# Differential and index scores in joint visits, upper and lower rows in turn

## The chip, the core and the metric

One core of a Trainium2 chip runs the whole kernel. The metric is the device time of one execution in microseconds, median of several; less is better.

## What is computed

Two layers of a decoder trunk on 256 tokens of width 2048, everything in float32. Each layer has a projection `w_in`, three kinds of attention heads side by side, an output projection, a cross attention and a feed-forward network. What matters here are the scores:

```python
# moba (6 heads, 128 wide) and dsa (6 heads, 128 wide): plain causal softmax attention,
# dsa only over the 64 keys that the index picks
# diff (4 heads): two components c of 64 columns each
sc = jnp.einsum('bqhcd,bshcd->bchqs', q, k) * scale
p = softmax(where(causal, sc, -inf))
a = p[:, 0] - lam * p[:, 1]
# index (8 heads of 64 columns): which keys dsa may see
rel = relu(jnp.einsum('bqhd,bsd->bqhs', qi, ki) * idx_scale)
score = jnp.einsum('bqhs,bqh->bqs', rel, w)
_, sel = lax.top_k(where(causal, score, -inf), 64)
```

With 256 tokens and blocks of 256, moba attends to its own block alone. There are 2 query tiles of 128 rows; tile `t = 0` sees 128 keys and tile `t = 1` sees 256 (`KW = (128, 256)`).

## The kernel before

**The main stream.** TensorE multiplies activations with streamed weights nearly all the time. A weight tile comes by DMA as float32 (`raw`, 4 buffers), ScalarE rounds it to a high half `hi` (L81, 4 buffers), VectorE forms the low half `lo = raw - hi` (L83, 3 buffers), and three matmuls replace one: `x_hi·hi`, `x_lo·hi`, `x_hi·lo` (L222, L223, L224 in `mm_rows` for the projections, L249 and L250 in `up_acc` for the rest). Outputs lie in 4 PSUM banks with the tag `mm`.

**The side work.** Everything about the heads (transposes, scores, softmax, products with the values, normalisation) is written as Python generators. `tick` (L159) is called by the main stream after every two blocks of `mm_rows`, or four of `up_acc`; it counts one and continues each generator that is due. `yield n` means "go on n ticks later". What a generator issues at one tick is called a visit below: on TensorE it stands between two matmuls of the main stream. The constants are in L32: `G_T` ticks from the end of a projection to its transposes, `G_S` from the transposes to the first scores, `G_PT` to the transposed probabilities, `G_DN` to the last transposes of the differential heads. Side work has 4 PSUM banks of its own, tag `at`, one for each call of `pat()`. The framework then orders every engine's instructions; an instruction that would wait can be placed a little behind main matmuls.

**Scores.** `softmax_pair` (L604) makes the scores of two units. For the plain heads a unit is one head with all 128 rows of contraction. For the differential heads a unit is one component `c` of one head: rows 0 to 63 of `qT` and `kT` for component 0, rows 64 to 127 for component 1. The second unit comes one tick after the first. Within a unit the two query tiles share one bank: matmul of `t = 0` (L618), masked maximum on VectorE (L620), then the same for `t = 1`. Since VectorE reads the bank that the second matmul writes, that matmul waits for the first L620.

**Index.** `index_masks` (L709) goes through the query tiles. The 8 index heads lie in four tiles of 128 rows, even heads in rows 0 to 63 and odd heads in rows 64 to 127. A group is four even or four odd heads for `t = 0`, two for `t = 1`, since 512 columns fill a bank. So there are 2 groups for `t = 0` and 4 for `t = 1`, each with a `yield 1`, a bank of its own, matmuls (L724), one Relu on ScalarE (L727) and a weighted sum on VectorE (L729).

**What follows.** 8 rounds of top-8 on VectorE (L734, L735) make the dsa mask, while the differential heads already run. After the last projection (`values(("mv", 2, 4))`, 8 ticks) the output projection `residual` starts; its first output block takes the mixed heads in the order 6 to 13, 14 and 15, 0 to 5 (one tick after each four blocks or at a group's end). Heads 4 and 5, the last moba pair, are its last operands. They come from `plain_pair`: product with the values (L665, L666), then `split` (L179: ScalarE L182, VectorE L186).

Of the kernel before, what the change touches and what calls it, by code (L numbers as in the profile page):

```python
# [13 lines left out]
AF = mybir.ActivationFunctionType  # L14
OP = mybir.AluOpType
AX = mybir.AxisListType

P = 128
D = 2048
S = 256  # L20
L = 2
NT = S // P
# [6 lines left out]
NEG = -1.0e30  # L29
GONE = -3.0e38  # L30
TOPK = 64
G_R, G_T, G_S, G_PT, G_DN = 5, 5, 1, 3, 3  # L32
FIRST_COL = 3328
KP, AP, RAWS, HIS, LOS = 38, 8, 4, 4, 3
SEVEN = frozenset((2, 5, 8, 11, 14, 16, 18))
# [8 lines left out]
def hybrid_trunk(ctx: ExitStack, tc: tile.TileContext, x, mem, positions, attn_norm, w_in,  # L44
# [3 lines left out]
    nc = tc.nc  # L48
# [9 lines left out]
    def slot(dt=F32):  # L58
        return kp.tile([P, CH], dt, tag="k", name="k", bufs=KP)
# [4 lines left out]
    def tmp():  # L64
        return tp.tile([P, CH], F32, tag="t", name="t", bufs=7)
# [4 lines left out]
    def pat():  # L70
        return ps.tile([P, CH], F32, tag="at", name="at")
# [41 lines left out]
    masks = [mask[:, P:], mask]  # L113
# [487 lines left out]
    KW = (P, S)  # L601
    PO = (0, P)

    def softmax_pair(units, mk, res, ri):  # L604


        mx = sp.tile([P, 2, NT], F32, tag="mx", name="mx")
        sm = sp.tile([P, 2, NT], F32, tag="sm", name="sm")
        for i, (qT, kT, lo, hi, sc) in enumerate(units):
            if i:  # L610
                yield 1
            pt = pat()
            s = tmp()
            p = slot()
            for t in range(NT):
                w = KW[t]
                o = pt[:, t * S:t * S + w]
                nc.tensor.matmul(o, lhsT=qT[lo:hi, t * P:(t + 1) * P], rhs=kT[lo:hi, :w],  # L618
                                 start=True, stop=True)
                nc.vector.tensor_tensor_reduce(out=s[:, PO[t]:PO[t] + w], in0=o, in1=mk[t], scale=1.0,  # L620
                                               scalar=GONE, op0=OP.add, op1=OP.max,
                                               accum_out=mx[:, i, t:t + 1])
            nb = sp.tile([P, NT], F32, tag="nb", name="nb")
            nc.vector.scalar_tensor_tensor(nb, mx[:, i, :], -1.0, sc, op0=OP.mult, op1=OP.mult)
            for t in range(NT):
                v = slice(PO[t], PO[t] + KW[t])
                nc.scalar.activation(p[:, v], s[:, v], AF.Exp, scale=sc[:, t:t + 1],
                                     bias=nb[:, t:t + 1], accum_out=sm[:, i, t:t + 1])
            res.append(p)
        nc.vector.reciprocal(ri, sm)  # L630
# [17 lines left out]
    def plain_pair(qTs, kTs, scs, mk, vs, mixT, base):  # L648

        while len(mk) < NT:  # L650
            yield 1
        prob, ri = [], new_ri()
        yield from softmax_pair([(qTs[i], kTs[i], 0, P, scs[i]) for i in range(2)], mk, prob, ri)
        for i in range(2):
            for t in range(NT):
                v = slice(PO[t], PO[t] + KW[t])
                nc.vector.tensor_scalar(prob[i][:, v], prob[i][:, v], ri[:, i, t:t + 1], None, op0=OP.mult)
        yield G_PT
        pTs = [p_T(prob[i]) for i in range(2)]
        yield 1  # L660
        while not vs():
            yield 1
        for i, v in enumerate(vs()):
            pt = pat()
            nc.tensor.matmul(pt[:, :S], lhsT=v[0], rhs=pTs[i][:, :S], start=True, stop=False)  # L665
            nc.tensor.matmul(pt[:, P:S], lhsT=v[1], rhs=pTs[i][:, S:3 * P], start=False, stop=True)  # L666
            mixT[base + i] = mix_slot(base + i)
            split((mixT[base + i], pt[:, :S], None))
# [40 lines left out]
    def index_masks(iqT, ikT, iw, res):  # L709

        accs = []
        for t in range(NT):
            w = KW[t]
            cur = slot()[:, :w]
            accs.append(cur)
            per = CH // w
            groups = [range(o, 8, 2) for o in range(2)]
            groups = [g[i:i + per] for i in range(0, 4, per) for g in groups]
            for hs in groups:
                yield 1  # L720
                pt = pat()
                for i, h in enumerate(hs):
                    lo = 64 * (h % 2)
                    nc.tensor.matmul(pt[:, i * w:(i + 1) * w], lhsT=iqT[h // 2][lo:lo + 64, t * P:(t + 1) * P],  # L724
                                     rhs=ikT[lo:lo + 64, :w], start=True, stop=True)
                rel = tmp()
                nc.scalar.activation(rel, pt, AF.Relu, scale=64 ** -0.5)  # L727
                for i, h in enumerate(hs):
                    nc.vector.scalar_tensor_tensor(cur, rel[:, i * w:(i + 1) * w], iw[t][:, h:h + 1],  # L729
                                                   masks[t] if h == 0 else cur, op0=OP.mult, op1=OP.add)  # L730
        for i in range(TOPK // 8):
            for cur in accs:
                m8 = sp.tile([P, 8], F32, tag="m8", name="m8")
                nc.vector.max(m8, cur)  # L734
                nc.vector.match_replace(out=cur, in_to_replace=m8, in_values=cur, imm_value=GONE)  # L735
            yield 1
        for t, cur in enumerate(accs):
            nc.vector.tensor_scalar(cur, cur, GONE / 2, None, op0=OP.is_gt)
            nc.vector.scalar_tensor_tensor(cur, cur, NEG, masks[t], op0=OP.mult, op1=OP.add)
        res += accs  # L740
# [38 lines left out]
    for l in range(L):  # L779
# [247 lines left out]
        def up_tiles(fs):  # L1027

            outs = up_acc(up, [(fs[0] * P, 2 * P)] if fs[1] == fs[0] + 1 else [(f * P, P) for f in fs], h3)
            res = []  # L1030
            uvs = [tmp() for _ in fs]
            for i, uv in enumerate(uvs):
                nc.scalar.activation(uv[:, S:], outs[i][:, S:], AF.Copy)  # L1033
            for i, f in enumerate(fs):
                u, v = uvs[i][:, :S], uvs[i][:, S:]
                nc.vector.tensor_tensor(u, outs[i][:, :S], v, OP.add)
                nc.vector.tensor_tensor(u, u, R, OP.mult)  # L1037
                nc.scalar.activation(v, u, AF.Identity, scale=cw[:, 2, f:f + 1], bias=cw[:, 3, f:f + 1])  # L1038
                nc.vector.scalar_tensor_tensor(v[:, 1:], u[:, :S - 1], cw[:, 1, f:f + 1], v[:, 1:],  # L1039
                                               op0=OP.mult, op1=OP.add)  # L1040
                nc.vector.scalar_tensor_tensor(v[:, 2:], u[:, :S - 2], cw[:, 0, f:f + 1], v[:, 2:],
                                               op0=OP.mult, op1=OP.add)
                res.append(v)
            return res
# [7 lines left out]
        for f in range(0, NF - 1, 2):  # L1052
            gs = up_tiles([f, f + 1])
# [3 lines left out]
        gs = up_tiles([NF - 1, 2 * NF - 1])  # L1057
# [8 lines left out]
        for g in range(D // GW):  # L1066
# [11 lines left out]
            for n in range(2):  # L1078
                for h in range(2):
                    i = 4 * g + 2 * n + h  # L1080
                    pt = pat()
# [39 lines left out]
```

## Time and profile before

| | |
|---|---|
| three runs | 2525.49, 2535.51, 2544.1 us; median 2535.51 us |
| the profiled execution | 2534.38 us, of which the span is 2532.6 us |
| TensorE busy | 2513.5 us (99% of the span) |
| TensorE weight loads | 2146.4 us (85%) |
| VectorE busy | 1918.0 us (76%) |
| ScalarE busy | 1383.5 us (55%) |
| mean granted TensorE clock | 0.998 of full speed |

A matmul's busy time in the profile runs on while the next has already started (the records overlap), so the distance from one start to the next tells more than the busy share. A float32 matmul of the side work appears as two records, each with its own weight load; the transposes and the main stream's matmuls are one record each. Shapes read rows*columns of the weights and then rows x columns of what streams: `64*128 64x256` is a matmul with 64 rows of contraction and 256 streamed columns.

### The profile page before, as it was taken

Reading aid. Unit: us, or ns where it says so; the run is one execution under the profiler, and the core shown is the slowest. Engines: PE = TensorE matmul, PEld = TensorE weight load, DVE = VectorE, ACT = ScalarE, POOL = GpSimd, SP = SyncE. Lnnn points to the kernel's source line nnn. Section 1 sums busy time; section 2 is a strip of 40 time slices with the busy share of each in tenths; the row PEclk is TensorE's granted clock in tenths of the full one; section 3 lists DMA queues with packets and bytes.
Section 4 is the critical chain, followed back from the end, with each engine's and each line's share of the span. In section 5 each row is a group of like instructions: output and inputs, shape, how many; then the busy total and the mean of one; then the engine's idle time right before and its main releaser. Section 6 shows DMA issues by size and latency. Waiting matters only on the chain.

```text
span 2532.6 us, 34711 instructions
## 1 busy us (share of the span) xinstructions
PE 2513.5 (99%) x13402; PEld 2146.4 (85%) x13402; DVE 1918.0 (76%) x3022; ACT 1383.5 (55%) x1784; POOL 168.4 (7%) x177
## 2 busy tenths in 40 slices
PE   8999999999999999999999999999999999999999
PEld 7778888898888888887897788888888888888887
DVE  7876767767777777889978767776776766768898
ACT  6555555555555555566545555554555555555654
POOL 2210101010000000000041011010100000000000
PEclk9999999999999999999999999999999999999999
DMA  8545556455666666555664454563666556664563
GB/s 269 160 146 177 161 159 200 162 185 184 184 193 189 187 195 184 174 191 194 218 191 158 152 166 154 166 221 126 191 191 186 184 184 187 191 187 159 196 235 125
DMA packets 378138, 459.90 MB, mean 182 GB/s; under 512 B 10686, under 2 KB 331764, under 8 KB 377972
## 3 DMA queue, kind: packets, MB, share of 16 engines
q1 hardware_dynamic: 377972, 457.68, 56.7%
q8 instruction: 105, 1.72, 0.3%
q14 instruction: 61, 0.50, 0.1%
HBM read 455.54 MB, written 2.10 MB: 181 GB/s over the span
## 4 chain that ended last, share of the span: by engine, by line
PE 95%; DVE 3%; DMA 1%; ACT 0%; issue 0%; SPq 0%; DVEq 0%; ACTq 0%
PE mm L249 30%; PE mm L250 16%; PE mm L222 9%; PE mm L223 9%; PE mm L224 9%; PE mm L289 5%; PE mm L287 5%; PE mm L288 5%; PE at L618 1%; DVE lo L83 1%; PE at L289 1%; PE at L287 1%; PE at L288 1%; PE at L593 1%; DMA k<-in_ffn_conv_b_dram 1%; DVE k L188 1%
## 5 line engine op out<-in xcount | busy, mean ns | idle before, releaser
L83 DVE TENSOR_TENSOR lo<-raw,hi 128x2048 fp32r<-128x2048 f32 (+3 forms) x522 | 1047.6, 2012 | 427.3 <-ACT t L1033 215.2
L249 PE MATMUL mm<-k,hi 128*128 128x512 f32 x3136 | 1109.5, 397 | 0.0
L81 ACT ACTIVATE hi<-raw 128x2048 fp32r<-128x2048 f32 (+3 forms) x522 | 866.1, 1670 | 367.2 <-PE mm L223 178.9
L250 PE MATMUL mm<-k,lo 128*128 128x256 f32 x3264 | 918.3, 281 | 0.0
L249 PEld LDWEIGHTS mm<-k,hi 128*128 128x128 f32 x3136 | 590.9, 188 | 136.2
L250 PEld LDWEIGHTS mm<-k,lo 128*128 128x128 f32 x3264 | 620.3, 190 | 0.3
L222 PE MATMUL mm<-hi,k 128*128 128x512 f32 (+2 forms) x1088 | 413.8, 380 | 0.0
L224 PE MATMUL mm<-lo,k 128*128 128x512 f32 (+2 forms) x1088 | 401.6, 370 | 0.8 <-DVE lo L83 0.8
L223 PE MATMUL mm<-hi,k 128*128 128x512 f32 (+2 forms) x1088 | 400.8, 368 | 0.0
L222 PEld LDWEIGHTS mm<-hi,k 128*128 128x128 f32 x1088 | 205.4, 189 | 37.0 <-issue 5.3
L224 PEld LDWEIGHTS mm<-lo,k 128*128 128x128 f32 x1088 | 204.7, 188 | 35.0 <-DVE lo L83 1.2
L223 PEld LDWEIGHTS mm<-hi,k 128*128 128x128 f32 x1088 | 205.7, 189 | 31.0 <-issue 2.0
L1033 ACT ACTIVATE t<-mm 128x256 f32<-128x256 f32 x172 | 65.1, 379 | 279.7 <-PE mm L250 279.7
L288 PE MATMUL mm<-hi,a 128*128 128x512 f32 x548 | 213.7, 390 | 0.1
L289 PE MATMUL mm<-lo,a 128*128 128x512 f32 x548 | 213.8, 390 | 0.0
L287 PE MATMUL mm<-hi,a 128*128 128x512 f32 x548 | 213.8, 390 | 0.0
L1038 ACT ACTIVATE t<-t,cw 128x256 f32<-128x256 f32 x172 | 94.2, 595 | 117.7 <-DVE t L1037 117.7
L410 POOL TENSOR_TENSOR k<-k,t 128x512 f32<-128x512 f32 x35 | 52.5, 1501 | 1124.0 <-ACT t L409 1123.7
L288 PEld LDWEIGHTS mm<-hi,a 128*128 128x128 f32 x548 | 103.0, 188 | 21.9 <-DVE a L271 0.6
L289 PEld LDWEIGHTS mm<-lo,a 128*128 128x128 f32 x548 | 103.0, 188 | 21.6 <-DVE lo L83 0.4
L287 PEld LDWEIGHTS mm<-hi,a 128*128 128x128 f32 x548 | 103.0, 188 | 20.9
L1039 DVE SCALAR_TENSOR_TENSOR t<-t,cw 128x255 f32<-128x255 f32 x172 | 82.6, 481 | 33.5 <-ACT t L1038 33.5
(230 smaller groups left out, 2386.2 us busy)
## 6 DMA issues: line engine op xcount, KB each, us to landing
raw<-in_ffn_w_up_dram SPq DMA_DIRECT2D x168, 1024.0 KB, 5.3
raw<-in_w_in_dram SPq DMA_DIRECT2D x152, 512.0 KB, 4.0
raw<-in_ffn_w_down_dram SPq DMA_DIRECT2D x56, 1024.0 KB, 5.5
raw<-in_w_in_dram SPq DMA_DIRECT2D x20, 1024.0 KB, 5.5
raw<-in_w_out_dram SPq DMA_DIRECT2D x16, 1024.0 KB, 5.6
raw<-in_cross_wkv_dram SPq DMA_DIRECT2D x16, 1024.0 KB, 5.2
raw<-in_ffn_w_down_dram SPq DMA_DIRECT2D x32, 512.0 KB, 5.6
raw<-in_ffn_w_down_dram SPq DMA_DIRECT2D x56, 256.0 KB, 3.9
```

Of the source, the lines that this page charges most:

```text
L81: nc.scalar.activation(hi[:, v, :], src[:, v, :], AF.Copy)
L83: nc.vector.tensor_tensor(lo[:, v, :], src[:, v, :], hi[:, v, :].bitcast(F32), OP.subtract)
L222: nc.tensor.matmul(o, lhsT=xh, rhs=hi[:, j, :], start=first, stop=False)
L223: nc.tensor.matmul(o, lhsT=xl, rhs=hi[:, j, :], start=False, stop=False)
L224: ins = nc.tensor.matmul(o, lhsT=xh, rhs=lo[:, j, :], start=False, stop=last)
L249: nc.tensor.matmul(outs[i], lhsT=wh, rhs=acts[k], start=first, stop=False)
L250: ins = nc.tensor.matmul(own[i], lhsT=wl, rhs=acts[k][:, :S], start=False, stop=last and (i == 1 or not whole))
L287: nc.tensor.matmul(bank[q], lhsT=x[0], rhs=w[0], start=first, stop=False)
L288: nc.tensor.matmul(bank[q], lhsT=x[1], rhs=w[0], start=False, stop=False)
L289: return nc.tensor.matmul(bank[q], lhsT=x[0], rhs=w[1], start=False, stop=left[q] == 0)
L1038: nc.scalar.activation(v, u, AF.Identity, scale=cw[:, 2, f:f + 1], bias=cw[:, 3, f:f + 1])
L1039: nc.vector.scalar_tensor_tensor(v[:, 1:], u[:, :S - 1], cw[:, 1, f:f + 1], v[:, 1:], op0=OP.mult, op1=OP.add)
```

## The change

The scores of both components of a differential head are issued in one visit into two banks, in the order `t = 0` component 0, `t = 0` component 1, `t = 1` component 0, `t = 1` component 1, so that rows 0 to 63 and rows 64 to 127 take turns. All score matmuls of a unit, those of plain heads too, now stand ahead of the VectorE work on them. Softmax work stays where it was: the second unit's still comes a tick later. In the index, an even and an odd group are formed in one visit into two banks, head by head in turn, every second tick. `G_T` goes from 5 to 6, for all transposes that follow a projection.

```diff
-G_R, G_T, G_S, G_PT, G_DN = 5, 5, 1, 3, 3
+G_R, G_T, G_S, G_PT, G_DN = 5, 6, 1, 3, 3
...
-        for i, (qT, kT, lo, hi, sc) in enumerate(units):
+        split_rows = units[0][2] != units[1][2]
+        pts = {}
+
+        def scores(todo):
+
+            for i in todo:
+                pts[i] = pat()
+            for t in range(NT):
+                for i in todo:
+                    qT, kT, lo, hi, _ = units[i]
+                    nc.tensor.matmul(pts[i][:, t * S:t * S + KW[t]], lhsT=qT[lo:hi, t * P:(t + 1) * P],
+                                     rhs=kT[lo:hi, :KW[t]], start=True, stop=True)
+
+        for i, unit in enumerate(units):
             if i:
                 yield 1
-            pt = pat()
+            if i not in pts:
+                scores(range(2) if split_rows else [i])
+            sc = unit[-1]
             s = tmp()
             p = slot()
             for t in range(NT):
                 w = KW[t]
-                o = pt[:, t * S:t * S + w]
-                nc.tensor.matmul(o, lhsT=qT[lo:hi, t * P:(t + 1) * P], rhs=kT[lo:hi, :w],
-                                 start=True, stop=True)
-                nc.vector.tensor_tensor_reduce(out=s[:, PO[t]:PO[t] + w], in0=o, in1=mk[t], scale=1.0,
-                                               scalar=GONE, op0=OP.add, op1=OP.max,
+                nc.vector.tensor_tensor_reduce(out=s[:, PO[t]:PO[t] + w], in0=pts[i][:, t * S:t * S + w],
+                                               in1=mk[t], scale=1.0, scalar=GONE, op0=OP.add, op1=OP.max,
                                                accum_out=mx[:, i, t:t + 1])
...
-            for hs in groups:
-                yield 1
-                pt = pat()
-                for i, h in enumerate(hs):
-                    lo = 64 * (h % 2)
-                    nc.tensor.matmul(pt[:, i * w:(i + 1) * w], lhsT=iqT[h // 2][lo:lo + 64, t * P:(t + 1) * P],
-                                     rhs=ikT[lo:lo + 64, :w], start=True, stop=True)
-                rel = tmp()
...
+            for gs in (groups[i:i + 2] for i in range(0, len(groups), 2)):
+                yield 2
+                pts = [pat() for _ in gs]
+                for i in range(per):
+                    for pt, hs in zip(pts, gs):
+                        lo = 64 * (hs[i] % 2)
+                        nc.tensor.matmul(pt[:, i * w:(i + 1) * w],
+                                         lhsT=iqT[hs[i] // 2][lo:lo + 64, t * P:(t + 1) * P],
+                                         rhs=ikT[lo:lo + 64, :w], start=True, stop=True)
+                for pt, hs in zip(pts, gs):
+                    rel = tmp()
...
```

## Rows read from the trace of the kernel before

**Rows 1.** The page of the profile: the span, its part 1 (busy us, share, instructions of each engine) and the row of the granted TensorE clock in 40 slices (9 is 90% or more).
```profile
span 2532.6 us, 34711 instructions
PE 2513.5 (99%) x13402; PEld 2146.4 (85%) x13402; DVE 1918.0 (76%) x3022; ACT 1383.5 (55%) x1784; POOL 168.4 (7%) x177
...
PEclk9999999999999999999999999999999999999999
```

**Rows 2.** Who waited for whom, TensorE matmuls alone, whole span: us in total, times, longest. The longest and the one of the score matmuls.
```profile
PE at L376 <- DMA k<-in_x_dram: 3.8, 5, 2.0
...
PE at L618 <- DVE mx L620: 0.9, 2, 0.5
```

**Rows 3.** Timeline of TensorE around the first and the third index visit of the first layer: start us, us, engine, line, tiles, shape, count of records merged.
```profile
82.36 0.39 PE L224 MATMUL mm<-lo,k 128*128 128x512 f32 x1
82.68 1.16 PE L724 MATMUL at<-k 64*128 64x128 f32 x8
...
84.10 0.39 PE L223 MATMUL mm<-hi,k 128*128 128x512 f32 x1
...
90.43 0.39 PE L224 MATMUL mm<-lo,k 128*128 128x512 f32 x1
90.75 1.13 PE L724 MATMUL at<-k 64*128 64x256 f32 x4
...
92.14 0.40 PE L223 MATMUL mm<-hi,k 128*128 128x512 f32 x1
```

**Rows 4.** Timeline of TensorE around two score matmuls of a differential component, `t = 0` and then `t = 1`, same columns.
```profile
110.04 0.39 PE L224 MATMUL mm<-lo,k 128*128 128x512 f32 x1
110.36 0.49 PE L618 MATMUL at<-k 64*128 64x128 f32 x2
...
111.11 0.39 PE L223 MATMUL mm<-hi,k 128*128 128x512 f32 x1
111.34 0.40 PE L224 MATMUL mm<-lo,k 128*128 128x512 f32 x1
111.67 0.70 PE L618 MATMUL at<-k 64*128 64x256 f32 x2
...
112.63 0.40 PE L223 MATMUL mm<-hi,k 128*128 128x512 f32 x1
```

**Rows 5.** Groups of TensorE instructions by line and shape, whole span: busy us, mean ns of a record, idle before. The 64-row scores.
```profile
L618 PE MATMUL at<-k 64*128 64x256 f32 x32 | 11.1, 429 | 0.9 <-DVE mx L620 0.9
...
L724 PE MATMUL at<-k 64*128 64x256 f32 x32 | 9.0, 403 | 0.0
...
L618 PE MATMUL at<-k 64*128 64x128 f32 x32 | 7.8, 323 | 0.0
...
L724 PE MATMUL at<-k 64*128 64x128 f32 x32 | 4.6, 285 | 0.0
```

**Rows 6.** Timeline of TensorE where the score matmuls of two components fall together (four records in one visit, merged under the first one's shape).
```profile
117.64 0.39 PE L224 MATMUL mm<-lo,k 128*128 128x512 f32 x1
117.96 0.70 PE L618 MATMUL at<-k 64*128 64x256 f32 x4
...
118.92 0.39 PE L223 MATMUL mm<-hi,k 128*128 128x512 f32 x1
```

**Rows 7.** The same stretch, 117.95 to 118.5 us, as groups by line and shape: which records these four are.
```profile
L618 PE MATMUL at<-k 64*128 64x256 f32 x2 | 0.7, 428 | 0.0
L618 PE MATMUL at<-k 64*128 64x128 f32 x2 | 0.5, 322 | 0.0
```

**Rows 8.** Timeline of TensorE: the one score matmul of a differential component that TensorE stood idle for, with what it waited for.
```profile
132.96 0.70 PE L618 MATMUL at<-k 64*128 64x256 f32 x2 [0.46 <-DVE mx L620]
```

**Rows 9.** Timeline of TensorE around the second score matmul of a plain head and the first one of the next head.
```profile
196.83 0.39 PE L223 MATMUL mm<-hi,k 128*128 128x512 f32 x1
197.10 0.70 PE L618 MATMUL at<-k 128*128 128x256 f32 x2
...
197.87 0.38 PE L618 MATMUL at<-k 128*128 128x128 f32 x2
...
198.33 0.40 PE L223 MATMUL mm<-hi,k 128*128 128x512 f32 x1
```

**Rows 10.** Timeline around the product with the values of the last moba pair: the product of head 4, then the first main matmul after it (on head 0) and the first on head 5, the last operand; and the two steps of `split` for head 5, on ScalarE and on VectorE.
```profile
363.03 0.60 PE L665 MATMUL at<-k 128*128 128x256 f32 x2
...
364.26 0.48 PE L249 MATMUL mm<-k,hi 128*128 128x512 f32 x1
...
365.37 0.41 ACT L182 ACTIVATE a<-at 128x256 fp32r<-128x256 f32 x1
...
366.44 0.42 DVE L186 TENSOR_TENSOR a<-at,a 128x256 fp32r<-128x256 f32 x1
...
367.87 0.40 PE L249 MATMUL mm<-a,hi 128*128 128x512 f32 x1
```

**Rows 11.** Busy time in stretches (us from the span's start): length, then busy us and instructions of each engine, granted clock, DMA share, GB/s. The stretch of the index's later groups, the top-8 rounds and the first differential heads in layer one, the one after it, and the same first stretch in layer two.
```profile
92.00:142.00 50.00, 49.54 (x223) 36.88 (x222) 47.28 (x143) 26.78 (x40) 6.08 (x5) 1.00 0.45 140
142.00:190.00 48.00, 48.00 (x217) 37.18 (x216) 34.98 (x92) 25.59 (x40) 4.05 (x4) 1.00 0.46 140
...
1346.00:1396.00 50.00, 49.54 (x223) 36.85 (x222) 47.09 (x143) 26.73 (x41) 5.73 (x5) 1.00 0.43 137
```

**Rows 12.** Timeline: a low half of weights being formed on VectorE, and the main matmul that is the first to read that tile.
```profile
121.02 2.29 DVE L83 TENSOR_TENSOR lo<-raw,hi 128x2048 fp32r<-128x2048 f32 x1
...
131.88 0.40 PE L224 MATMUL mm<-lo,k 128*128 128x512 f32 x1
```

More of the change, by code (lines that the diff above doesn't have):

```diff
@@ L718, in index_masks @@
             groups = [g[i:i + per] for i in range(0, 4, per) for g in groups]
-            for hs in groups:
-                yield 1
-                pt = pat()
-                for i, h in enumerate(hs):
-                    lo = 64 * (h % 2)
-                    nc.tensor.matmul(pt[:, i * w:(i + 1) * w], lhsT=iqT[h // 2][lo:lo + 64, t * P:(t + 1) * P],
-                                     rhs=ikT[lo:lo + 64, :w], start=True, stop=True)
-                rel = tmp()
[L727 to L730, printed above, removed]
+            for gs in (groups[i:i + 2] for i in range(0, len(groups), 2)):
[9 more added lines that the diff above has]
+                    rel = tmp()
+                    nc.scalar.activation(rel, pt, AF.Relu, scale=64 ** -0.5)
+                    for i, h in enumerate(hs):
+                        nc.vector.scalar_tensor_tensor(cur, rel[:, i * w:(i + 1) * w], iw[t][:, h:h + 1],
+                                                       masks[t] if h == 0 else cur, op0=OP.mult, op1=OP.add)
         for i in range(TOPK // 8):
```

## The prediction

> **What bounds the kernel now.** I read the page first: TensorE is busy for 99% of the span, at the full granted clock in all slices, and VectorE for 76% [rows 1]. Busy time of overlapping records can hide gaps, so the next view is who waited for whom on TensorE: in the whole span no wait but those for loads adds up to a microsecond, the longest being 3.8 us for the first input [rows 2]. The reader is to see that nobody makes TensorE wait: its own list of matmuls is the bound, and a visit of side work costs what it adds to that list. The third view is therefore the timeline of TensorE around each kind of visit, where I measure a visit as the start of the second main matmul behind it less the start of the last one before it, less two main steps. A main step is 0.23 us (111.11 to 111.34 [rows 4]). I take the second one behind because the first comes late and hands its delay on.
>
> **What a 64-row visit costs.** Index, eight records of 128 columns: 84.10 − 82.36 − 0.46 = 1.28 us; four of 256: 92.14 − 90.43 − 0.46 = 1.25 [rows 3]. Differential, two of 128: 111.11 − 110.04 − 0.46 = 0.61; two of 256: 112.63 − 111.34 − 0.46 = 0.83 [rows 4]. Six records of 128 more cost 0.67 more, so a record is 0.11; two of 256 more cost 0.42, so it is 0.21; and what is left in all four cases is 0.39 to 0.41. So each visit pays a fixed 0.40 us however short it is, and streams 0.22 (`t = 0`) or 0.42 (`t = 1`) for each score matmul. Plain heads pay no such sum (next part).
>
> **Do rows 0 to 63 and 64 to 127 run side by side?** The trace has one place that tells. At 117.96 two records of 256 and two of 128 columns stand in one visit, which can only be the second tile of one component and the first of the other [rows 6, 7]. It costs 118.92 − 117.64 − 0.46 = 0.82 us, as much as the lone 256 with its 0.83 [rows 4]: the other matmul came free. One after the other it would have been 0.40 + 0.42 + 0.22 = 1.04.
>
> **The change, part by part.**
>
> *Differential scores.* 32 records of each width over two layers [rows 5], two to a matmul, are 8 of each width in a layer. Now: 8 × 0.61 + 8 × 0.83 = 11.5 us, less 0.6 for the free one, plus 0.46 of a real wait in one visit, where the matmul of `t = 1` stood behind L620 of its own bank [rows 8]: 11.4 a layer. After: four visits, each with both components; side by side 0.40 + 0.22 + 0.42 = 1.04, together 4.2; one after the other 0.40 + 1.28 = 1.68, together 6.7. Saved: 7.2 a layer, at the least 4.7. I take the upper value, since [rows 6] is this very pairing. In two layers 14.4 us. The wait for L620 goes with it: no VectorE read stands between the matmuls of a bank any more, and what is late next is L620 itself, which waits for the later matmul, with nothing of TensorE behind it.
>
> *Index.* Now 2 × 1.28 + 4 × 1.25 = 7.6 a layer. After, three visits: side by side 1.28 + 2 × 1.25 = 3.8; one after the other (0.40 + 16 × 0.11) + 2 × (0.40 + 8 × 0.21) = 6.3. Saved 3.8 a layer, at the least 1.3; I take 3.8, in two layers 7.6.
>
> *Plain heads.* The `t = 1` matmul, which came behind L620, moves up to its `t = 0`. From 196.83 to 198.33 stand three main steps (0.69) and two score matmuls (0.64): 0.17 us too many [rows 9], because a matmul that waits for a semaphore starts late and the next too. 12 pairs of plain heads in two layers: 0 to 2 us saved; I take 2.0, as the row shows it.
>
> *Vector and scalar work.* L620, L727 and L729 are the same in number and shape: nothing added or removed. No DMA is added or moved.
>
> *`G_T` at 6.* One tick later for all transposes costs TensorE nothing in the middle, where other heads' visits and main matmuls fill the tick. At the end it does. The last moba pair's product now comes on tick 11 after its projection: 8 ticks of the last projection, then three of the first output block (two in heads 6 to 13, one behind 14 and 15). With one tick more it moves inside heads 0 to 5, behind head 3, and heads 4 and 5 are read next. Now the row from the product (363.03) to the end of head 5's `split` (366.44 + 0.42) is 3.8 us, covered by four heads of main work [rows 10]. Then the cover is only the product itself (364.26 − 363.03 = 1.2). Queued behind those waiting matmuls is all of TensorE. Price: between nothing (if the order puts other ready matmuls there) and 3.8 − 1.2 = 2.6 a layer; part of the 3.8 is the turn of the memory tiles, which then lies a tick earlier, so I take 1.0 a layer, 2.0 in both.
>
> *The sum.* 14.4 + 7.6 + 2.0 − 2.0 = 22.0 us off the profiled execution's own 2534.4: **2512 us**. That execution stands 1.1 us below the median of the three runs (2535.5), so against the median it is −0.9%.
>
> **A rule to weigh here.** The row shows 0.40 us at each entry and exit of 64-row work [rows 3, 4], and no such sum inside the visit of both halves [rows 6]. The Trainium skill ("TensorEngine Tiling (Array Packing)", Key Properties) says that changing the tiling mode drains the engine and that changing only the tile does not. The trace agrees, with the 0.40 and the 0.82. By the rule the 25 changes of half that I count below cost nothing, and the sum stays; were each a drain, the third rival would hold.
>
> **The rivals.**
>
> 1. *The halves don't overlap in long visits.* [Rows 6] shows one pair of matmuls, not eight in turn, and matmuls with two records each may queue. For it: nothing more than that. Then the least savings hold: 9.4 + 2.6 + 2.0 − 2.0 = 12.0, **2522 us**. That half the visits break apart because two banks aren't free at once gives about the same: half of what overlap brings (2.5 + 2.5 a layer) is 5 us, half of what joining alone brings is 6, and 22 − 11 = 11 leaves 2523.
>
> 2. *VectorE becomes the bound of a stretch.* From 92 to 142 us it is busy 47.3 of 50 us, in layer two 47.1 [rows 11], so it could give up only 2.7. TensorE would save some 6.1 there: four index visits become two (2.5), and the two heads of the first pair become two visits (3.6). If TensorE then stands for the difference, 3.4 a layer go: 15 saved, **2519 us**. Against it: the low halves run far ahead; the tile that VectorE ended at 123.31 is first read at 131.88, 8.6 us later [rows 12], more than the 7.4 saved by then (3.8 of the index, 3.6 of the heads). After 142 VectorE has 13 us of 48 free [rows 11]. The Trainium skill ("TensorEngine Tiling (Array Packing)", PSUM Bottleneck and Gotcha 1) warns that tiling speeds up TensorE but not the evacuation, and that row tiles press on PSUM. Two of four banks in one visit, the second one read only a tick later behind a saturated VectorE, is how it would show here; in the trace of before no wait for a bank stands among TensorE's waits.
>
> 3. *Slower: each change of half is a drain.* If the 0.40 belongs to any change of the row group, the turns are the worst order. Changes inside visits: 4 × 3 for the heads, 7 + 3 + 3 for the index, 25 a layer, 10.0 us; nothing overlaps, so the least savings stand against it, 6.0 a layer. That is 4.0 a layer lost: **2542 us**. It turns the sign from 0.24 us a change on. Against it: the 0.82 of [rows 6].
>
> **Chances.** Forecast 0.70 (its own range 2503 to 2521: the unknown ends of `G_T` and of the plain heads are 2510 to 2516, and the three runs lie 9 to 10 us either side of their median), first rival 0.12, second 0.14, third 0.04. The range reaches over the first two with the runs' own scatter: 2502 to 2528. A change of 1% (25 us, 2510 against the median) is about what a measurement of this kernel can tell from none. The forecast lies 2 us inside it, so some four in ten of its 0.70 fall below, with nearly nothing from the rivals: faster 0.30; slower would need 0.74 us a change in the third rival: 0.03; within 1%: 0.67.
>
> **What would show it.** In the profile after: four L618 visits of 64 rows a layer, eight records each, at some 1.04 us by the measure above, and three L724 visits at 1.28 and 1.25. 1.68 and over 2 would mean rival 1. The wait of L618 for L620 is gone. TensorE's waits gain a row, for `lo` L83 or a bank, if rival 2 holds; a main matmul late behind L665 and L666 after the last projection shows the price of `G_T`. The forecast is wrong if the first layer's output projection doesn't start some 11 to 12 us earlier than now, or if it does and the time comes back in the rest, which nothing in the change touches.

## The result and the profile after

| | before | after |
|---|---|---|
| median, 7 executions each | 2542.46 us (2525.49 to 2545.13) | 2517.99 us (2508.24 to 2519.28) |
| the profiled execution | 2534.38 us | 2517.99 us |
| ratio of the times, on record | | 0.992, 95% interval [0.9901, 0.9939] |

The changed kernel is 1.0% faster by the medians, 0.8% by the ratio on record and 0.65% by the two profiled executions (16.4 us). The profiles are the better comparison, since executions of either kernel fall into groups 9 us apart in both kernels alike: in each layer one stage, the up projection of the feed-forward network, runs as a whole at one of two steps (last section). Both profiled executions have one layer at each step, while four of the seven executions of before have the slower one in both, as their times tell. "At equal steps" means below: corrected for that, 9.2 us a layer.

The page of the kernel after: span, part 1, row of the granted clock.

```profile
span 2516.2 us, 34714 instructions
...
PE 2492.8 (99%) x13402; PEld 2139.5 (85%) x13402; DVE 1913.7 (76%) x3022; ACT 1381.0 (55%) x1784; POOL 166.4 (7%) x177
...
PEclk9999999999999999999999999999999999999999
```

Nothing has changed at this height against [rows 1]: TensorE is still at 99%. The stages tell more. Their lengths, from the start of a stage's first main matmul to that of the next stage's:

| us | before, layer 1 / 2 | after, layer 1 / 2 | difference |
|---|---|---|---|
| heads (`mm_rows`, to the first L249) | 342.03 / 340.91 | 332.71 / 332.29 | −9.3 / −8.6 |
| output projection | 95.76 / 95.76 | 96.66 / 96.31 | +0.9 / +0.55 |
| a stage of the cross attention | 26.00 / 26.00 | 26.28 / 26.28 | +0.3 / +0.3 |
| up projection | 508.74 / 520.46 | 517.70 / 510.98 | −0.5 in both together |

The sum is −16.4. The heads give 17.9, where the visits alone should have given 24. The visits themselves, timeline of TensorE around the first index visit, a differential visit and a plain one of the kernel after (start us, us, engine, line, tiles, shape, records):

```profile
88.84 0.39 PE L224 MATMUL mm<-lo,k 128*128 128x512 f32 x1
89.16 1.16 PE L737 MATMUL at<-k 64*128 64x128 f32 x16
...
90.59 0.39 PE L223 MATMUL mm<-hi,k 128*128 128x512 f32 x1
...
109.95 0.39 PE L224 MATMUL mm<-lo,k 128*128 128x512 f32 x1
110.27 0.93 PE L619 MATMUL at<-k 64*128 64x128 f32 x8
...
111.46 0.39 PE L223 MATMUL mm<-hi,k 128*128 128x512 f32 x1
...
189.07 0.39 PE L224 MATMUL mm<-lo,k 128*128 128x512 f32 x1
189.30 0.82 PE L619 MATMUL at<-k 128*128 128x128 f32 x4
...
190.19 0.39 PE L223 MATMUL mm<-hi,k 128*128 128x512 f32 x1
```

By the prediction's measure the index visit costs 90.59 − 88.84 − 0.46 = 1.29 us with sixteen records, where [rows 3] had 1.28 with eight. The differential visit costs 1.05 with both components. The plain one costs 0.66, its 0.64 of streaming and next to nothing else. So in the visits TensorE does what was forecast, and most of what is missing is a wait. TensorE's waits after, whole span (us in total, times, longest), and the place in layer one on the timeline:

```profile
PE mm L224 <- DVE lo L83: 5.4, 3, 2.3
...
PE at L1001 <- DVE k L992: 0.7, 2, 0.4
```

```profile
128.90 0.50 PE L224 MATMUL mm<-lo,k 128*128 128x512 f32 x1 [2.34 <-DVE lo L83]
...
1382.44 0.50 PE L224 MATMUL mm<-lo,k 128*128 128x512 f32 x1 [2.33 <-DVE lo L83]
```

The first row is far above its 0.8 us in the kernel before. Of its 5.4 us, 0.7 lie at the start of the kernel, as before, and 2.3 in each layer (the second line is layer two's): the main stream itself stands still for a low half of weights. The row for L620 is gone. In layer two the wait costs more than itself. The windows right behind it in either layer (length, then PE, PEld, DVE, ACT, POOL, and the granted clock third from the end):

```profile
128.90:132.30 3.40, 3.40 (x18) 2.89 (x19) 3.40 (x16) 0.74 (x3) 0.00 (x0) 1.00 0.65 183
1383.20:1386.60 3.40, 3.40 (x10) 2.57 (x10) 3.40 (x12) 0.00 (x0) 0.00 (x0) 0.50 0.92 283
```

In layer two TensorE is granted 0.50 of its clock for these 3.4 us, 1.2 instead of 2.4 GHz, and gets through 10 records instead of 18. From the matmul that waited to the same matmul of the list, 60 main matmuls on, it takes 19.27 us in layer one and 20.83 in layer two: the half clock costs 1.56 us. VectorE in windows from 92 us to this wait, and in layer two likewise (columns as in [rows 11]: length, then PE, PEld, DVE, ACT, POOL), and then its timeline ahead of layer one's low half:

```profile
92.00:129.00 37.00, 34.66 (x169) 26.67 (x167) 36.61 (x131) 22.20 (x33) 3.30 (x5) 1.00 0.31 100
1346.00:1383.00 37.00, 34.67 (x168) 26.67 (x167) 36.61 (x131) 22.38 (x33) 2.83 (x5) 1.00 0.32 96
```

```profile
114.20 2.28 DVE L83 TENSOR_TENSOR lo<-raw,hi 128x2048 fp32r<-128x2048 f32 x1
...
118.23 1.22 DVE L692 TENSOR_SCALAR k<-k,ri 128x128 f32<-128x128 f32 x2
119.36 0.74 DVE L693 SCALAR_TENSOR_TENSOR k<-k,ri 128x128 f32<-128x128 f32 x2
120.02 1.27 DVE L583 TENSOR_REDUCE sq<-t 128x8 f32<-128x512 f32 x2
121.21 0.68 DVE L566 TENSOR_TENSOR k<-k 128x512 f32<-128x512 f32 x1
...
126.56 2.28 DVE L83 TENSOR_TENSOR lo<-raw,hi 128x2048 fp32r<-128x2048 f32 x1
```

VectorE is busy for 36.61 of the 37 us in both layers: up to the wait it has next to no slack. Between two low halves (114.20 and 126.56) stand top-8 rounds, the mix of a differential head (L692, L693), the rotations of other heads (L583, L566) and the masked maxima of both components. This tile was done at 123.31 before and read at 131.88 [rows 12]. Now it is done at 128.85, 5.5 us later, and wanted at 128.90 − 2.34 = 126.56, 5.3 us earlier. That eats the 8.6 us of lead and 2.3 more. In the kernel before, the mix (there L680, L681) and the same rotations stood behind this low half, on VectorE's timeline:

```profile
123.69 0.55 DVE L680 TENSOR_SCALAR k<-k,ri 128x128 f32<-128x128 f32 x2
...
128.11 1.27 DVE L583 TENSOR_REDUCE sq<-t 128x8 f32<-128x512 f32 x2
```

All of VectorE's work is no larger than before (1913.7 us against 1918.0 [rows 1]); what has changed is what stands ahead of this tile. The second rival has come, with a price of 2.3 us a layer and the half clock in one. Whether the amount of VectorE's work in the stretch would do it in any order is for the experiments to tell.

### The profile page after: what moved, and what is told of

Same layout as the page of the kernel before. It is cut to its first block, busy times and chain, and to the rows that moved or that the text cites. A ratio compares the mean times of both kernels' runs of the same rounds, so it can differ in the third digit from the quotient of the medians.

```text
span 2516.2 us, 34714 instructions
## 1 busy us (share of the span) xinstructions
PE 2492.8 (99%) x13402; PEld 2139.5 (85%) x13402; DVE 1913.7 (76%) x3022; ACT 1381.0 (55%) x1784; POOL 166.4 (7%) x177
## 4 chain that ended last, share of the span: by engine, by line
PE 92%; DVE 5%; DMA 1%; issue 1%; ACT 0%; SPq 0%; ACTq 0%; DVEq 0%
PE mm L249 31%; PE mm L250 16%; PE mm L222 8%; PE mm L224 8%; PE mm L223 8%; PE mm L289 5%; PE mm L288 5%; PE mm L287 5%; DVE lo L83 2%; PE at L289 1%; PE at L287 1%; PE at L288 1%; PE at L619 1%; DMA k<-in_ffn_conv_b_dram 1%; PE at L593 1%
## 5 line engine op out<-in xcount | busy, mean ns | idle before, releaser
L249 PE MATMUL mm<-k,hi 128*128 128x512 f32 x3136 | 1109.4, 396 | 0.0
L249 PEld LDWEIGHTS mm<-k,hi 128*128 128x128 f32 x3136 | 589.8, 188 | 137.7 <-DVE k L186 0.5
```

The costliest lines, as they stand in the source:

```text
L249: nc.tensor.matmul(outs[i], lhsT=wh, rhs=acts[k], start=first, stop=False)
```

## Experiments

E1 to E7 were run once each (E2 a second time). Within a group, executions of one kernel differ by up to some 3 us, so less than that is read from stages and not from the whole time.

**E1: all 64-row matmuls read rows 0 to 63.** Does the gain of the visits come from two halves running side by side?

```diff
-                    qT, kT, lo, hi, _ = units[i]
+                    qT, kT, lo, hi, _ = units[i if not split_rows else 0]
...
-                        lo = 64 * (hs[i] % 2)
+                        lo = 0
```

> The changed kernel, but every 64-row score matmul reads rows 0 to 63 (component 0 twice, each even index head twice), so that the visits, banks and counts stay and only the turns of the halves are gone; the scores of component 1 and of the odd index heads are thus not computed. Theory (the halves stream side by side): without them a head's visit costs 0.40 + 1.28 = 1.68 us instead of 1.06, index visits 2.16 and 2.08 instead of 1.29 and 1.27, that is 5.0 us more in a layer; the 2.3 us for which TensorE stands for a low half near 128 us shrink as it arrives later, so the first matmul of the output projection comes 2.7 to 5.0 us later than 343.98. Rival (joining the visits did it all): the visits stay at 1.06 and 1.27 and the start stays within 0.5 us.

One execution took 2531.69 us, with the slower step in both layers, which is 4.5 us more than the kernel after would have so. The first index visit on TensorE's timeline:

```profile
88.15 0.39 PE L224 MATMUL mm<-lo,k 128*128 128x512 f32 x1
88.47 2.05 PE L737 MATMUL at<-k 64*128 64x128 f32 x16
...
90.79 0.39 PE L223 MATMUL mm<-hi,k 128*128 128x512 f32 x1
```

It costs 2.18 us (1.29 with both halves), the two others 2.12 and 2.12 (1.26), the differential ones 1.70 (1.05). These are the streams in a row plus the fixed 0.40, so the overlap of the halves is shown. The visits grew by 5.2 us a layer, but the heads' stretch by only 2.7 and 1.8: the wait for the low half shrank to 1.6 us in all, and no stretch of the heads has the half clock. A faster TensorE had run into it; a slower one runs out of it.

**E2: halves not in turn, but one after the other within a visit.** The same matmuls, first all lower rows, then all upper rows.

```diff
-            for t in range(NT):
-                for i in todo:
+            for i in todo:
+                for t in range(NT):
...
-                for i in range(per):
-                    for pt, hs in zip(pts, gs):
+                for pt, hs in zip(pts, gs):
+                    for i in range(per):
```

> The changed kernel, but within a visit all matmuls of the lower half come first and then all of the upper half (component 0 with both query tiles, then component 1; all even heads, then all odd ones). Theory (matmuls of the two halves overlap only where they are neighbours in the list): a head's visit costs about 1.5 to 1.7 us, the long index visit about 2.1. Rival (the engine looks far enough ahead to find the other half): 1.06 and 1.29 as with turns, so that the order within the visit would not matter.

The one execution took 7342.31 us and says nothing of the edit: its main stream ran slowly from the first matmul on (0.84 us a step between 12 and 90 us instead of 0.23), ahead of every edited line. The same kernel again:

> The same kernel as with the halves grouped within a visit. Theory (matmuls of the two halves overlap only where they are neighbours in the list): a head's visit 1.5 to 1.7 us, the long index visit about 2.1. Rival (the engine looks far enough ahead): 1.06 and 1.29.

2528.19 us, with the slower step in both layers, about 1 us more than the kernel after would have so. Its first index visit (sixteen records) and its second (eight):

```profile
88.15 0.39 PE L224 MATMUL mm<-lo,k 128*128 128x512 f32 x1
88.47 1.71 PE L737 MATMUL at<-k 64*128 64x128 f32 x16
...
90.45 0.39 PE L223 MATMUL mm<-hi,k 128*128 128x512 f32 x1
...
95.47 0.39 PE L224 MATMUL mm<-lo,k 128*128 128x512 f32 x1
95.79 1.14 PE L737 MATMUL at<-k 64*128 64x256 f32 x8
...
97.20 0.40 PE L223 MATMUL mm<-hi,k 128*128 128x512 f32 x1
```

With eight records, four of each half, the visit costs 1.27 us, as with turns; the differential ones cost 1.06, as with turns. Only the long visit, eight records of one half ahead of eight of the other, costs 1.84 us, between 1.29 (turns) and 2.18 (same rows). So what pays is that both halves stand in one visit. The turns themselves matter in one visit a layer, by 0.55 us.

**E3: the kernel after with five ticks, and E4: the kernel before with six.** What does `G_T` do alone? E3 is the edit below, E4 the reverse one on the kernel before.

```diff
-G_R, G_T, G_S, G_PT, G_DN = 5, 6, 1, 3, 3
+G_R, G_T, G_S, G_PT, G_DN = 5, 5, 1, 3, 3
```

> The changed kernel with G_T back at 5. Theory (the extra tick costs at the end of the heads alone): the output projection, 96.66 and 96.31 us from its first matmul to the next stage, goes back to the 95.76 of before, a gain of 0.9 and 0.6, and the heads' stretch before it stays within 1 us of 332.7. Rival (the extra tick pays somewhere in the heads' stretch, by spreading VectorE's work): that stretch grows by more than 1 us, and TensorE's wait for low halves by as much.

> The kernel before with G_T at 6 and nothing else. Theory (the tick spreads VectorE's work, which in the kernel before makes TensorE wait for 0.5 us a layer only): the heads' stretch stays within 1 us of 342.0 and 340.9, and the output projection grows by 0.6 to 0.9 us, so the tick by itself brings nothing. Rival (the tick is worth several us by itself): the heads' stretch shrinks by 2 us or more.

The kernel after with five ticks: 2516.67 us with the faster step in both layers, 6 to 8 us more than the kernel after at equal steps (2508 to 2511). The output projection is back at 95.76 us, but the heads take 337.64 and 336.17, 4.9 and 3.9 more. The wait for the low half is gone from the layers. A longer one stands in its place, on TensorE's timeline:

```profile
135.77 0.48 PE L647 MATMUL at<-ident,k 128*128 128x128 f32 x1 [5.64 <-DVE k L693]
```

The transposes of the differential probabilities wait for their mix on VectorE. And the stall has an echo, in the windows right behind it (columns as in [rows 11], the clock third from the end):

```profile
135.00:139.00 4.00, 3.23 (x15) 3.23 (x16) 1.85 (x9) 0.58 (x2) 0.00 (x0) 0.50 1.10 357
139.00:142.00 3.00, 3.00 (x23) 2.32 (x21) 0.56 (x1) 2.90 (x6) 0.00 (x0) 0.96 0.16 49
```

For some 3.5 us after it TensorE is granted 0.50 of its clock. The kernel before with six ticks: 2539.05 us against 2534.4 at equal steps, so the tick alone costs 2.3 us a layer: 1.05 and 1.13 in the heads (0.45 a layer of it a longer wait for L620), 1.4 and 1.3 in the output projection, 0.3 each in the cross attention. It costs something by itself, and it pays only together with the joint visits. Whether it pays by giving VectorE time is for E9 to test.

**E5 to E7: the top-8 rounds moved by ticks.** If VectorE has too much to do at once, spread its top-8 rounds or begin them later.

```diff
# E5: a round every second tick
-            yield 1
+            yield 2
# E6: the first round 8 ticks later
+        yield 8
         for i in range(TOPK // 8):
# E7: E6, with G_T back at 5
```

> The changed kernel with the eight rounds of top-8 two ticks apart instead of one. Theory (TensorE stands 2.3 us a layer for a low half because VectorE is full between 92 and 142 us, and the rounds are what can be put off): the wait of L224 for L83 falls from 5.4 us to under 1, and the first matmul of the output projection comes 2 us earlier than 343.98, in both layers, 4 us in all. Rival (what delays the low half is the work of the second pair's rotation and of two components' softmax behind one visit): the wait stays at 1.5 us a layer or more.

> The changed kernel with all eight rounds of top-8 begun eight ticks later, when the first pair of differential heads has left VectorE; the mask is still ready ten ticks before the first dsa scores. Theory (VectorE holds more than fits between 92 and 142 us, and every wait there, for a low half or for the mixed probabilities of L693, is its backlog): both waits are gone in both layers (each under 0.5 us), and the first matmul of the output projection comes at 341.0 to 341.7 instead of 343.98, 2.3 us or a little more. Rival (the waits come from the order in which VectorE's work is placed, not from its amount): a wait of 2 us or more shows up at another place, as it did with the rounds two ticks apart.

> As before with late rounds, and G_T at 5. Theory (the sixth tick only bought VectorE time): with the backlog gone the 5.6 us wait of L647 for L693, seen with G_T at 5, is under 1 us, the first matmul of the output projection stays within 0.7 us of the run with late rounds, and the output projection takes 95.76 again instead of 96.7 and 96.3. Rival (the sixth tick covers the chain of softmax itself, which is longer than the ticks between scores and transposes): 3 us or more of that wait stay.

2522.87, 2522.33 and 2516.03 us; at equal steps some 5, 4 and 5 to 8 us slower than the kernel after (E5 and E6 had one layer at each step, E7 the faster step in both). TensorE's longest wait by the profile of E5:

```profile
PE at L647 <- DVE k L693: 6.6, 2, 3.3
```

In all three the wait for the low half is gone from the layers and the transposes wait for the mix instead: 3.3 us a layer in E5 and E6, 5.6 in E7. In E6 VectorE's list still has ten of the sixteen top-8 instructions (L734 in the kernel before, two to a round) at 107 to 116 us, where they stood in the kernel after; the last five, at 114 to 126 us there, came at 130 to 136. So the tick at which a generator is continued binds TensorE's instructions more than VectorE's, which takes much of what is ready, and the ticks moved only the end of what they were meant to move.

**E8 and E9: the rounds tied behind the mix on VectorE's own list.** The top-8 instructions may stand only behind the mix of the first differential pair.

```diff
+                mix = nc.vector.scalar_tensor_tensor(prob[0][:, v], ...)
...
+            if i:
+                mixed.append(mix.ins)
...
+        n = len(mixed)
+        while len(mixed) == n:
+            yield 1
...
+                with tc.issue_after(mixed[n]):
                     nc.vector.max(m8, cur)
# E9: the same, with G_T back at 5
```

> The changed kernel with the rounds of top-8 tied behind the last mixing step (L693) of the first pair of differential heads on VectorE's own list. Beginning them later in the generator had not moved them: VectorE's list still had them between 107 and 116 us, since an instruction whose inputs are ready is placed where VectorE is free. Theory (VectorE's backlog makes the waits): now neither a low half nor L693 is waited for, the first matmul of the output projection comes at 341.0 to 341.8 instead of 343.98 in layer one and as much earlier in layer two, and the whole time is 4 to 5 us less than the changed kernel's at equal steps of the up projection. Rival (the chain of softmax, rotation and low halves is itself as long as the ticks): 2 us or more of waiting stay in a layer.

> The same with G_T at 5. Theory (the sixth tick only bought VectorE time): the wait of L647 for L693 falls from 5.6 to under 1 us a layer, the first matmul of the output projection comes within 0.7 us of that with the sixth tick, and the output projection takes 95.8 instead of 96.7 and 96.3. Rival (with five ticks the second pair's rotation falls between the first pair's scores and its mixing, whatever else VectorE does): 3 us or more of the wait stay, and the sixth tick is worth more than it costs.

E8: median 2517.22 us of 10, ratio to before 0.9929 [0.9907, 0.9951]; E9: 2514.3 us of 10, 0.9938 [0.9918, 0.9959]. At equal steps both are where the kernel after is (2508 to 2511 and 2517 to 2520), and the 4 to 5 us expected of E8 did not come. TensorE's wait in E8 (whole span) and its place:

```profile
PE at L648 <- DVE k L694: 4.4, 2, 2.2
```

```profile
132.15 0.33 PE L648 MATMUL at<-ident,k 128*128 128x128 f32 x1 [2.23 <-DVE k L694]
```

VectorE's timeline ahead of it (lines one higher than in the kernel after: L694 is the mix):

```profile
110.82 0.29 DVE L633 CUSTOM_DVE_ANT_0 t<-at,mask 128x128 f32<-128x128 f32 x1 [2.18 <-PE at L620]
...
113.83 2.29 DVE L83 TENSOR_TENSOR lo<-raw,hi 128x2048 fp32r<-128x2048 f32 x1 [1.54 <-PE mm L225]
...
124.56 2.28 DVE L83 TENSOR_TENSOR lo<-raw,hi 128x2048 fp32r<-128x2048 f32 x1
...
128.85 2.26 DVE L83 TENSOR_TENSOR lo<-raw,hi 128x2048 fp32r<-128x2048 f32 x1
...
131.29 0.55 DVE L693 TENSOR_SCALAR k<-k,ri 128x128 f32<-128x128 f32 x2
131.75 0.74 DVE L694 SCALAR_TENSOR_TENSOR k<-k,ri 128x128 f32<-128x128 f32 x2
```

With the rounds out of the way VectorE had caught up: it stood idle for 2.18 us up to 110.82 and for 1.54 up to 113.83. From there to the mix it worked through, and in those 18 us it formed two low halves that TensorE reads only at 138.48 and 145.01. Each delays the mix once. Behind the first one came the bias of the softmax, and ScalarE waited for it on its timeline:

```profile
127.03 0.49 ACT L640 ACTIVATE k<-t,nb,sc 128x128 f32<-128x128 f32 x1 [1.61 <-DVE nb L637]
```

The second one (128.85) stood between the sums of the softmax and the mix. So here the wait is read as one of order: an old backlog of VectorE would have gone with the rounds. No run has the two low halves behind the mix, so this is argued from the timeline and not shown. In E9 the waits are shorter and more (2.7, 1.8 and 1.7 us in two layers), and the heads take 334.50 and 332.35: with the rounds held, five ticks are as good as six in the whole time. That fits a sixth tick that buys VectorE time, though not in full: the wait for the mix fell from 5.6 to 1.4 us a layer and not below 1, and the first output projection starts 1.0 us later than in E8, not within the 0.7 expected.

**E10 and E11: the transposes of the differential probabilities a tick later**, in E10 on top of E8, in E11 on the kernel after.

```diff
-        yield G_PT - 1
+        yield G_PT
```

> The kernel with the top-8 rounds behind the differential mix, and the transposes of the differential probabilities taken one tick later (G_PT instead of G_PT - 1). Theory (the last waits of TensorE in the heads come from the order of VectorE's list: two low halves stand ahead of the mix at 131.75 us, and the transposes come 2.2 us a layer too early for it): the wait of the transposes for the mix falls from 4.4 us in all to under 1, each layer's heads' stretch gets about 2 us shorter than 333.4 and 332.1 us, and the time at equal steps of the up projection is about 4 us under the changed kernel's (2504 to 2506 and 2513 to 2515 where that has 2508 to 2511 and 2517 to 2519). Rival (VectorE's list leaves no slack, a wait taken away there comes back elsewhere): the low half that stands behind the mix, read 1.8 us after it is done, is late instead, or the tick itself costs about a us a layer at the end as the sixth tick did in the kernel before, and the stretch stays within 0.7 us of 333.4 and 332.1; the time stays in the same two groups.

> The changed kernel with only the transposes of the differential probabilities one tick later, the top-8 rounds left where they are. Theory (order of VectorE's list): the low half at 126.56 us stays behind the top-8 rounds and the rotations, so the wait of the main matmul for it stays near 2.3 us a layer, and the heads' stretch stays within 1 us of 332.7 and 332.3 us. Rival (it is the tie to the mix that matters, whatever stands ahead): with the mix less urgent the low half moves ahead of it, its wait falls under 1 us a layer and the stretch gets 2 us shorter.

E10: median 2525.39 us of 12, ratio to before 0.9966 [0.9943, 0.9989]; E11: 2523.64 us of 12, 0.9957 [0.9935, 0.9978]. At equal steps they are about 7 and 6 us slower than the kernel after. In E10 the wait for the mix is gone, and the one for the low half is only that of the start. The next step in the row is late. TensorE's timeline, VectorE's ahead of it, and the window behind it:

```profile
153.29 0.63 PE L719 MATMUL at<-ident,k 128*128 128x128 f32 x4 [3.50 <-DVE nb L637]
```

```profile
147.87 2.29 DVE L83 TENSOR_TENSOR lo<-raw,hi 128x2048 fp32r<-128x2048 f32 x1
150.07 0.15 DVE L177 SCALAR_TENSOR_TENSOR rs_y<-rs_u,rs_y 128x4 f32<-128x4 f32 x1
...
152.47 0.68 DVE L715 TENSOR_TENSOR k<-k,rs_y 128x512 f32<-128x512 f32 x1
```

```profile
154.00:158.00 4.00, 4.00 (x12) 3.17 (x11) 2.62 (x4) 2.32 (x8) 0.00 (x0) 0.59 0.40 122
```

The normalisation of the first pair (L177 to L715), which the transposes L719 read, stands behind another low half and shares VectorE with the next mix (the profile names L637, but L715, which ends at 153.15, is what they read). TensorE stands for 3.5 us in each layer, and in layer one the clock falls to half behind it (0.59 in the window shown). At the next pair's L719 another 1.5 and 1.9 us are lost. So the rival on record, that a wait taken away comes back elsewhere, is right, and dearer than it said. In E11 the wait for the low half stayed where it was (2.34 us, then at 128.69), as the theory of the order has it. The heads took 335.52 and 334.35 us, 2.8 and 2.1 more, not within the 1 us expected: the normalisation is late there too, by 1.5 and 1.9 us at the last transposes (L716), and the wait for the low half is followed by half clock in both layers, where the kernel after has it in layer two alone. None of the eleven kernels beats the kernel after at equal steps.

## Why the prediction came out as it did

The time was inside the range and within 1% of before. That range reached over the first two rivals too, so the hit says little about the mechanism. Of 22.0 us forecast, 16.4 came. The test that the text set itself, a first output projection some 11 to 12 us earlier, came out short: 353.15 − 343.98 = 9.2 us. By that sign the forecast was wrong: the gain of the visits was right, and the path from there to the time was not.

*Differential scores, −14.4: right.* Four visits a layer at 1.05 us (forecast 1.04); the fourth shares its visit with four transposes, 1.49 us together.

*Index, −7.6: right.* Visits of 1.29, 1.26 and 1.26 us (forecast 1.28 and 1.25). E1 shows what the overlap brings in heads and index: 5.2 of the 11.0 us a layer; the rest comes from joining the visits. So the first rival, which would have left the visits at 1.68 and over 2, falls.

*Plain heads, −2.0: right.* The 0.17 us too many [rows 9] are gone: each of the 24 plain visits costs some 0.66 us.

*`G_T`, +2.0: right in its size where it was looked for, and incomplete.* The output projections cost 0.90 + 0.55 = 1.45 us more. The 0.3 us a layer in the cross attention are the tick's too: that stage takes 26.00 us in each kernel with five ticks (before, E3, E7, E9) and 26.28 or 26.29 in the others. Together that is the 2.0 forecast, in part at a place where it wasn't looked for. How it comes about is open: layer one has 0.8 of its 0.9 us by the end of the first output block, as the text has it, but no wait of TensorE is listed there. E3 showed what the text didn't ask: with five ticks the heads take 8.8 us more, so the tick brings 3.4 us a layer net of its price. It belongs to the change.

*The third rival (each change of half a drain) falls.* 25 changes of half a layer cost nothing that can be seen: the visits stay at 0.40 plus one half's streams. The Trainium skill ("TensorEngine Tiling (Array Packing)", Key Properties) says that changing only the tile does not drain the engine. The trace agrees, with the 1.05.

*The step that failed is the dismissal of the second rival.* "VectorE becomes the bound of a stretch" had 0.14, and the text set a lead of 8.6 us [rows 12] against 7.4 us saved, with VectorE's own times taken as given. They weren't: the same low half was formed 5.5 us later, because the work of both components and of other heads now comes ready earlier and stood ahead of it. The wait is 2.3 us a layer, 4.7 in all, where the rival had 3.4 a layer. The text also put nothing in its sum for what a stall does to the clock: 1.56 us in layer two. So the measured 2518.0 lies beside the rival's 2519 and not beside 2512; that it lies within 1 us is luck, since the wait is smaller than the rival's and the terms below fill up the rest. The rival's picture, that VectorE's amount of work sets the difference, fits the kernel after (36.61 of 37 us) and not E8, where a wait as long comes 18 us after idle time: which piece of work stands ahead in VectorE's list decides as much. The Trainium skill ("TensorEngine Tiling (Array Packing)", PSUM Bottleneck) warns that the evacuation doesn't get faster with the matmuls. The trace agrees in part: it was VectorE, but it showed as a late low half of weights, and no wait for a bank stands among TensorE's waits.

*What is left.* 24.0 us were forecast in the heads and 17.9 came. The waits take 4.7 of the difference and the half clock 1.6. Another 0.9 was lost in layer one ahead of every changed line: the first matmuls take 0.42 us a step instead of 0.23 until about 12.4 us in the profiled execution of before and 14.5 in that of after. That makes 7.2 where 6.1 are missing, so the rest of the heads brought 1.1 us more than forecast, about as much in either layer (0.6 and 0.5). Which part did was not taken apart. Whether another order of VectorE's list, with the early low halves behind both the mix and the normalisation, would take the 2.3 us away was not tried.

## What to carry to other kernels

Work on 64 rows of contraction paid a fixed price for each visit here (0.40 us), so bring both halves and as many matmuls as the banks allow into one visit; the exact turn of the halves matters only when many of one half stand ahead of the other. When a faster engine shares a helper with others, the lead that a trace shows is no promise: ask what the scheduler will put ahead of the late piece once everything comes ready earlier. And judge a constant such as `G_T` with the change and without it, since here it costs 2.3 us a layer alone and brings 3.4 together with the rest.

## What the runs showed of the hardware

**Two steps of one stage.** The up projection is 1376 pairs of a 512-column and a 256-column matmul in each layer, with nothing between most of them. Two stretches of the kernel after, in layer one and in layer two, six pairs apart:

```profile
699.81 0.40 PE L249 MATMUL mm<-k,hi 128*128 128x512 f32 x1
...
701.93 0.40 PE L249 MATMUL mm<-k,hi 128*128 128x512 f32 x1
...
1999.67 0.39 PE L249 MATMUL mm<-k,hi 128*128 128x512 f32 x1
...
2001.75 0.39 PE L249 MATMUL mm<-k,hi 128*128 128x512 f32 x1
```

2.12 us against 2.08, which is 353.3 ns a pair against 346.7, at the full granted clock in both. 1376 × 6.67 ns = 9.2 us. The kernel before has the two steps in the opposite layers. The executions of every kernel that was run several times lie in groups about that far apart (19 of before beside E8: six at 2524.8 to 2526.7, ten at 2533.4 to 2535.4, three at 2543.1 to 2544.0 us). What chooses the step stays open. A change worth less than 9 us is read from profiles whose steps are known, or from the groups, and not from a median of few.

**Half clock behind a stall.** Nine kernels stood still in both layers' heads, for 2.2 to 5.6 us (the kernel after, E2, E3, E5 to E8, E10, E11). In sixteen of these eighteen places the granted clock fell to half, 1.2 GHz, during the stall or up to 1.4 us after it. In the two others it stayed at full: behind 2.34 us in layer one of the kernel after, and behind 3.5 us in layer two of E10. The kernel after had the same stall in layer two with the fall, so the length of a stall alone doesn't decide. The price there was 1.56 us on top of the stall.

**Halves overlap though they are not neighbours in the list.** In one visit, four records of one half ahead of four of the other overlap as well as in turns (1.27 us against 1.26); eight of 128 columns ahead of eight overlap only in part (1.84 against 1.29, E2).
